# A layer kernel of matrix products: how the first weight slabs are fetched, and what TensorE does until they are there

## The chip, the cores and the metric

The program runs on one core of one Trainium2 chip. The metric is the device time of one execution in microseconds (us); a shorter time is better. The core's engines named here are TensorE (PE in the rows, with its weight loads as PEld), VectorE (DVE), ScalarE (ACT), GpSimd (POOL) and SyncE (SP), which does nothing here but issue transfers (DMA) from the chip's memory (HBM) into the core's own.

## What is computed

One layer over 256 positions of width 2048: an RMS norm, one wide projection, two mixers that run over it in both directions (an mLSTM and a gated DeltaNet), a gated merge with a residual sum, and a feed-forward block of width 8192. Cut from the reference:

```python
def reference(x, norm1_g, w_in, ..., w_branch_m, w_branch_d, w_out, norm2_g, w_ff1, w_ff2, norm_f_g):
    for l in range(DEPTH):                                  # DEPTH = 1
        h = _rms_norm(x, norm1_g[l])
        proj = h @ w_in[l]                                  # 256 x 2048 times 2048 x 11312
        (m_q, m_k, m_v, m_o, m_i, m_f, d_qkv, d_z, d_a, d_b, gates) = jnp.split(proj, split_points, axis=-1)
        y_m = _mlstm_mixer(m_q, m_k, m_v, m_o, m_i, m_f, ...)       # 4 heads
        y_d = _gated_deltanet_mixer(d_qkv, d_z, d_a, d_b, ...)      # conv of 5 taps, 8 heads
        g_m, g_d = jnp.split(gates, 2, axis=-1)
        mixed = jax.nn.sigmoid(g_m) * (y_m @ w_branch_m[l]) + jax.nn.sigmoid(g_d) * (y_d @ w_branch_d[l])
        x = x + mixed @ w_out[l]
        h = _rms_norm(x, norm2_g[l])
        x = x + jnp.square(jax.nn.relu(h @ w_ff1[l])) @ w_ff2[l]
    return _rms_norm(x, norm_f_g)
```

All inputs and the output are float32.

## The kernel before

**Products in three parts.** A large product of float32 is made of three faster ones: each operand is split into a rounded part (`wh`, `xTh`, type fp32r) and the rest (`wl`, `xTl`), and TensorE adds `wh` times `xTh`, `wl` times `xTh` and `wh` times `xTl`. The weights are split on the chip as they arrive, slab by slab.

**Slabs.** A slab (class `Gran`, lines 271 to 299) is two tiles of 128 rows of a weight matrix over one chunk of columns: 288 columns in the first chunk, 512 in nearly all others. SP fetches it into one of NR = 3 buffers `raw` (L286); ScalarE casts it into one of NW = 4 buffers `wh`; VectorE subtracts that from `raw` into `wl`; TensorE then makes 12 products of it: two row tiles, two tiles of positions, three parts. `gemm` (L301) builds the slabs of a chunk, `drive` (L342) runs all slabs of the program in one list. The split of slab i + 3 (its fetch included) is written half-way through the products of slab i. A fetch into `raw` waits until VectorE has read the slab that had the same buffer three slabs earlier.

**The start.** The first chunk is `zab` (288 columns, slabs 0 to 7). Its slabs carry two more steps: `x_load` fetches the rows of the transposed input into `xtr` behind each slab (L382), and `x_prep` (L385) makes `xTh` on ScalarE and `xTl` on VectorE, two operations each a slab, scaled with the norm's gains, which lie in `pr`. `pr` is the first transfer on SP (L379). The second chunk (`d`, 512 columns, slabs 8 to 15) carries `xn_load`: a piece `xn` of the untransposed input behind each slab (L407), and behind the last one the constants `cs`.

**Side work.** Everything that is not a slab is written as tasks: `x_norm` squares the pieces of `xn` into a scratch tile `junk` and makes the root `r1` (its task yields eight squares, a table load and the root on ScalarE, four small steps on VectorE); the chunks `d` are then scaled into `tmd` on ScalarE and transposed by TensorE into `ptd`, and so on through the convolution, both mixers and the gates. A planner places them: `_Clocks` keeps a modelled time for each engine, and at each half slab `pump` takes the tasks whose modelled start is near TensorE's (`pick`). A slab's modelled arrival (`arrive`, in `split`) goes into these times, so it moves the places of side work. The order that comes out is fixed: each engine runs its instructions in the order in which they were written (`keep_in_program_order`), recorded by one helper (L108), so that most rows of the trace carry its line, and the tile's name tells what they are.

**The mLSTM heads.** Much later, around slabs 103 to 112, the heads' scores `sp` are masked into `mm` on VectorE and multiplied on TensorE into `nf` and `nb`, from which VectorE makes `hm`; at the same stretch GpSimd adds masks and VectorE still has every slab's `wl` to make.

Of the kernel before, what the change touches and what calls it, by code (L numbers as in the profile page):

```python
# [9 lines left out]
F32 = mybir.dt.float32  # L10
# [6 lines left out]
P = 128  # L17
# [17 lines left out]
HOP = 0.1  # L35
XNW = 6.0

NR, NW = 3, 4

LIM = dict(T=9, V=2, A=1.2, G=3)  # L40
TABLES = {AF.Sigmoid: "sigmoid", AF.Exp: "exp", AF.Ln: "ln", AF.Sqrt: "sqrt"}
# [98 lines left out]
def layer_kernel(ctx, tc, x, xt, cst, prm, w_in, w_bm, w_bd, w_out, w_ff1, w_ff2, gf, out):  # L140
    nc = tc.nc
    clk = _Clocks()
    V, A, T, G = (_Ordered(tc, e, k, clk) for e, k in
                  ((nc.vector, "V"), (nc.scalar, "A"), (nc.tensor, "T"), (nc.gpsimd, "G")))
# [8 lines left out]
    wp = ctx.enter_context(tc.tile_pool(name="wp", bufs=1))  # L153
# [117 lines left out]
    class Gran:  # L271


        def __init__(self, src, shape, mms, us, pre=None, post=None, prep=None, load=None, segs=2):
            self.src, self.shape, self.mms, self.us = src, shape, mms, us
            self.pre, self.post, self.prep, self.load, self.segs = pre, post, prep, load, segs

        def split(self, i):
            n = int(np.prod(self.shape))
            raw = wp.tile([P, 1024], F32, tag="raw", name="raw", bufs=NR)  # L280
            self.wh = wp.tile([P, 1024], F32R, tag="wh", name="wh", bufs=NW)
            self.wl = wp.tile([P, 1024], F32R, tag="wl", name="wl", bufs=NW)
            rv = raw[:, :n]
            if len(self.shape) == 2:
                rv = rv.rearrange("p (k c) -> p k c", k=self.shape[0])
            nc.sync.dma_start(out=rv, in_=self.src)  # L286
            arrive = (GR[i - NR].ready if i >= NR else 0.0) + 2.3
            arrive = max(arrive, GR[i - 1].arrive if i else 0.0) + n * 512 / 360e3
            if self.load:
                arrive += self.load()  # L290
            self.arrive = arrive
            free = GR[i - NW].end if i >= NW else 0.0
            clk.t["A"] = max(clk.t["A"], free, arrive)
            A.copy(self.wh[:, :n], raw[:, :n])
            clk.t["V"] = max(clk.t["V"], clk.t["A"] + HOP)
            V.tensor_sub(self.wl[:, :n], raw[:, :n], self.wh[:, :n].bitcast(F32))
            if self.prep:
                self.prep()
            self.ready = clk.t["V"] + HOP

    def gemm(w, c0, cw, lh, ll, kt, name, evac, needs=None, pre=None, prep=None, load=None):  # L301

        box = {}

        def mk(g):
            def mms(gr):
                if g == 0:
                    while left["acc"] < 2:
                        force()
                    left["acc"] -= 2  # L310
                    box["ps"] = [ps_acc.tile([P, 512], F32, tag="acc", name=f"{name}_{i}") for i in range(2)]
                for kk in range(2):
                    for t in range(2):
                        k = g + kk
                        ws = slice(kk * cw, (kk + 1) * cw)
                        ts_ = slice(t * P, (t + 1) * P)
                        o = box["ps"][t][:, :cw]
                        h, l = lh()[:, k, ts_], ll()[:, k, ts_]
                        T.matmul(o, h, gr.wh[:, ws], start=(k == 0), stop=False)
                        T.matmul(o, h, gr.wl[:, ws], start=False, stop=False)  # L320
                        T.matmul(o, l, gr.wh[:, ws], start=False, stop=(k == kt - 1))
                    if kk == 0:
# [12 lines left out]
            src = w[g * P:(g + 2) * P, c0:c0 + cw].rearrange("(k p) c -> p k c", p=P)  # L335
            return Gran(src, [2, cw], mms, 12 * cw / 2400 * 1.0125, pre_, post,
                        (lambda: prep(g)) if prep else None, (lambda: load(g)) if load else None)

        for g in range(0, kt, 2):
            GR.append(mk(g))  # L340

    def drive():  # L342
        for i in range(min(LA, len(GR))):
            GR[i].split(i)
        for i, gr in enumerate(GR):
            if gr.pre:
                gr.pre()
            t0 = max(clk.t["T"], gr.ready)
            clk.t["T"] = t0
            seg = gr.us / gr.segs  # L350
            parts = gr.mms(gr)
            gr.end = t0 + gr.us
            for j in range(gr.segs):
                clk.quiet = True
                next(parts, None)
                clk.quiet = False
                clk.t["T"] += seg
                if j == 0 and i + LA < len(GR):
                    pump()
                    gr.end = clk.t["T"] + seg * (gr.segs - 1)  # L360
                    GR[i + LA].split(i + LA)
# [14 lines left out]
    xTh = pa.tile([P, KT, S], F32R, tag="A0", name="xTh")  # L376
    xTl = pa.tile([P, KT, S], F32R, tag="A1", name="xTl")
    xtr = pm.tile([P, KT, S], F32, tag="ba", name="xtr")
    nc.sync.dma_start(out=pr, in_=prm)  # L379

    def x_load(g):
        nc.sync.dma_start(out=xtr[:, g:g + 2, :], in_=xt[:, g:g + 2, :])  # L382
        return 0.75

    def x_prep(g):  # L385
        for k in (g, g + 1):
            A.activation(xTh[:, k, :], xtr[:, k, :], AF.Copy, scale=g1c[:, k:k + 1])
        clk.t["V"] = max(clk.t["V"], clk.t["A"] - 0.3)
        for k in (g, g + 1):
            V.scalar_tensor_tensor(xTl[:, k, :], xtr[:, k, :], g1c[:, k:k + 1], xTh[:, k, :].bitcast(F32),  # L390
                                   op0=ALU.mult, op1=ALU.subtract)

# [2 lines left out]
    NX = DM // 512  # L395
    xl = []

    def xn_load(g):

        i = g // 2  # L400
        if i == 0:
            for t in range(2):
                xn[t] = pm.tile([P, DM], F32, tag=("yd", "hm")[t], name=f"xn{t}")
        t, j = i % 2, i // 2
        if j < NX:
            c = slice(j * 512, j * 512 + 512)
            nc.sync.dma_start(out=xn[t][:, c], in_=x[t * P:(t + 1) * P, c])  # L407
            xl.append(clk.t["A"])
        if g == KT - 2:
            nc.sync.dma_start(out=cs, in_=cst[:, :K_N])  # L410
            return 2.0
        return 0.73
# [7 lines left out]
    def x_norm():  # L420
        ss1 = small.tile([P, 2, NX], F32, name="ss1")
        v = small.tile([P, 2], F32, name="v1")
        junk = pm.tile([P, 512], F32, tag="cm", name="junk")
        for i in range(2 * NX):
            while len(xl) <= i:
                yield None
# [985 lines left out]
    def ff2_gran(pas, ks, ns, last=False, tail=False):  # L1412
# [26 lines left out]
                        mm(g_, ks_, k, 1)  # L1439
                start(ff2_end(1), "end1")  # L1440

        def prep():
# [212 lines left out]
```

## Time and profile before

| | before |
|---|---|
| device time, median of 3 runs (lowest to highest) | 1496.76 us (1496.39 to 1499.19) |
| the profiled execution's own time | 1496.8 us |
| its span in the profile | 1495.0 us |
| TensorE busy, share of the span | 1475.8 us, 99% |
| TensorE's weight loads (beside its products) | 1219.8 us, 82% |
| VectorE | 898.0 us, 60% |
| ScalarE | 781.5 us, 52% |
| GpSimd | 63.4 us, 4% |

The profiled execution took 1.8 us more than its span, which lies around the span and not in it. A share of 99% is a mean over the whole run: it says that an engine is nearly always at work, but not where the rest is lost. That is read from the list of its waits, and for the places it names from a timeline (each instruction with its start, its length and what ended the idle time ahead of it) and from windows (busy time of each engine in a stretch, the granted clock, the share of the 16 DMA engines and the bytes moved).

### The profile page before, as it was taken

The numbers are of one execution on the slowest core, as the hardware profiler recorded it, in microseconds if no ns is written. First come the engines' busy times: TensorE is split into PE (matmuls) and PEld (weight loads), VectorE is DVE, ScalarE is ACT, GpSimd is POOL, SyncE is SP. The second block draws the span as 40 slices with busy tenths as digits, with TensorE's granted clock in tenths as the row PEclk, the third lists the DMA queues.
The fourth block names the chain that finished last, engine by engine and source line by source line (L and its number), as shares of the span: only waits on it lengthen the run. The fifth ranks groups of instructions, "written<-read, shape, count | busy, mean of one in ns | idle before, by whom it ended". The sixth has DMA issues, their size and how long they took to land.

```text
span 1495.0 us, 19315 instructions
## 1 busy us (share of the span) xinstructions
PE 1475.8 (99%) x7196; PEld 1219.8 (82%) x7196; DVE 898.0 (60%) x1292; ACT 781.5 (52%) x1124; POOL 63.4 (4%) x101
## 2 busy tenths in 40 slices
PE   8999999999999999999999999999999999999997
PEld 7888788887878888887888888888888888888886
DVE  5658785368678836565555544454445555555875
ACT  5876545365765455443554444444445444444664
POOL 0020101012001100000000000000000000000000
PEclk9999999999999999999999999999999999999999
DMA  8766477464657754776656666666666666666564
GB/s 290 213 202 199 135 200 213 118 206 145 193 170 203 253 164 127 222 254 235 204 183 194 186 180 188 184 183 195 183 184 186 195 195 191 194 194 194 187 198 140
DMA packets 139805, 286.95 MB, mean 192 GB/s; under 512 B 9588, under 2 KB 18036, under 8 KB 139072
## 3 DMA queue, kind: packets, MB, share of 16 engines
q1 hardware_dynamic: 134816, 267.09, 60.1%
q0 software_dynamic: 4896, 18.64, 3.9%
q8 instruction: 56, 0.92, 0.2%
q14 instruction: 37, 0.30, 0.1%
HBM read 278.32 MB, written 7.36 MB: 191 GB/s over the span
## 4 chain that ended last, share of the span: by engine, by line
PE 90%; DVE 3%; DMA 3%; ACT 2%; issue 1%; DVEq 0%; SPq 0%; ACTq 0%
PE f L108 23%; PE y L108 23%; PE gm L108 6%; PE d L108 6%; PE gd L108 5%; PE wo L108 5%; PE mv L108 3%; PE bd L108 3%; PE bm L108 3%; PE z L108 2%; DMA raw<-in_w_in_dram 2%; PE mq L108 1%; PE mk L108 1%; DVE wl L108 1%; ACT wh L108 1%
## 5 line engine op out<-in xcount | busy, mean ns | idle before, releaser
L108 DVE TENSOR_TENSOR wl<-raw,wh 128x1024 fp32r<-128x1024 f32 (+3 forms) x512 | 611.3, 1196 | 534.2 <-ACT wh L108 533.0
L108 ACT CAST wh<-raw 128x1024 fp32r<-128x1024 f32 (+3 forms) x512 | 523.5, 1026 | 548.4 <-PE y L108 155.0
L108 PE MATMUL f<-wh,h2h 128*128 128x512 f32 x512 | 200.8, 392 | 0.0
L108 PE MATMUL f<-wh,h2l 128*128 128x512 f32 x512 | 199.5, 390 | 0.0
L108 PE MATMUL f<-wl,h2h 128*128 128x512 f32 x512 | 199.2, 389 | 0.0
L108 PE MATMUL y<-wh,ah 128*128 128x512 f32 x512 | 178.5, 389 | 0.0
L108 PE MATMUL y<-wl,ah 128*128 128x512 f32 x512 | 178.5, 389 | 0.0
L108 PE MATMUL y<-wh,al 128*128 128x512 f32 x512 | 178.3, 389 | 0.0
L108 PEld LDWEIGHTS f<-wh,h2l 128*128 128x128 f32 x512 | 96.1, 188 | 20.2
L108 PEld LDWEIGHTS y<-wh,al 128*128 128x128 f32 x512 | 96.1, 188 | 20.0
L108 PEld LDWEIGHTS y<-wl,ah 128*128 128x128 f32 x512 | 96.1, 188 | 20.0
L108 PEld LDWEIGHTS y<-wh,ah 128*128 128x128 f32 x512 | 96.0, 188 | 19.8
L108 PEld LDWEIGHTS f<-wl,h2h 128*128 128x128 f32 x512 | 96.2, 188 | 19.5
L108 PEld LDWEIGHTS f<-wh,h2h 128*128 128x128 f32 x512 | 96.1, 188 | 19.3
L108 PE MATMUL d<-wh,xTh 128*128 128x512 f32 x192 | 78.0, 406 | 0.0
L108 PE MATMUL d<-wl,xTh 128*128 128x512 f32 x192 | 75.2, 391 | 0.6 <-DVE wl L108 0.6
L108 PE MATMUL d<-wh,xTl 128*128 128x512 f32 x192 | 74.9, 390 | 0.0
L108 PE MATMUL gd<-wl,xTh 128*128 128x512 f32 x128 | 50.2, 392 | 1.8 <-DVE wl L108 1.7
L108 PE MATMUL wo<-wh,mTh 128*128 128x512 f32 x128 | 50.6, 395 | 0.2 <-ACT wh L108 0.2
L108 DVE TENSOR_TENSOR al<-aT,ah 128x256 fp32r<-128x256 f32 x128 | 50.8, 417 | 0.0
L108 PE MATMUL wo<-wl,mTh 128*128 128x512 f32 x128 | 50.0, 391 | 0.8 <-DVE wl L108 0.8
L108 PE MATMUL gm<-wh,xTh 128*128 128x512 f32 x128 | 50.6, 395 | 0.0
(316 smaller groups left out, 2153.3 us busy)
## 6 DMA issues: line engine op xcount, KB each, us to landing
raw<-in_w_ff_dram SPq DMA_DIRECT2D x256, 512.0 KB, 4.3
raw<-in_w_in_dram SPq DMA_DIRECT2D x160, 512.0 KB, 3.9
raw<-in_w_out_dram SPq DMA_DIRECT2D x32, 512.0 KB, 4.3
raw<-in_w_bm_dram SPq DMA_DIRECT2D x16, 512.0 KB, 4.2
raw<-in_w_bd_dram SPq DMA_DIRECT2D x16, 512.0 KB, 4.3
raw<-in_w_in_dram SPq DMA_DIRECT2D x16, 256.0 KB, 2.8
mx<-dgm POOLq DMA_DIRECT2D x4, 1024.0 KB, 6.2
raw<-in_w_in_dram SPq DMA_DIRECT2D x8, 288.0 KB, 4.3
```

The source lines that it names most:

```text
L108: return self._tc.keep_in_program_order(f(*a, **k))
```

## The change

The change rewrites how the first slabs are fetched, and adds products of zeros.

- `split` is taken apart: `fetch` issues a slab's transfers, `split` casts and subtracts. `drive` calls `fetch` for the first NF = 8 slabs (the first chunk) ahead of everything else, and with them their `x_load`.
- Slabs 0 to 2 use the three `raw` buffers, slabs 3 to 7 a tile `far` of their own (five slabs of 576 elements a partition) under the tag `cm`, which `junk` had; `junk` gets the tag `pk`.
- Slab 0 is fetched, cast, subtracted and prepared in two halves (one tile of 128 rows each).
- `pr` is issued on ScalarE's queue.
- VectorE sets a tile `zw` of 512 columns to zero, and TensorE runs nine float32 products of 128 x 128 zeros into `zp` ahead of its first real one.
- The planner's model of arrivals is changed with it: the first eight slabs have no wait for a buffer in it.

```diff
+NF = 8
...
+        def fetch(self, i):
+            n = int(np.prod(self.shape))
+
+            if NR <= i < NF:
+                self.raw = far[:, i - NR, :n]
+            else:
+                self.raw = wp.tile([P, 1024], F32, tag="raw", name="raw", bufs=NR)[:, :n]
...
+            arrive = 2.3 + (0.0 if i < NF else GR[i - NF].ready if i < NF + NR else GR[i - NR].ready)
+            arrive = max(arrive, GR[i - 1].arrive if i else 0.0)
+
+            self.at = []
+            for ks in ((0,), (1,)) if i == 0 else ((0, 1),):
+                if i == 0:
+                    nc.sync.dma_start(out=rv[:, ks[0], :], in_=self.src[:, ks[0], :])
+                else:
+                    nc.sync.dma_start(out=rv, in_=self.src)
+                lo, hi = (ks[0] * n // 2, (ks[0] + 1) * n // 2) if i == 0 else (0, n)
+                arrive += (hi - lo) * 512 / 360e3
+                if self.load:
+                    arrive += self.load(ks)
+                self.at.append((ks, lo, hi, arrive))
+            self.arrive = arrive
+
         def split(self, i):
-            n = int(np.prod(self.shape))
-            raw = wp.tile([P, 1024], F32, tag="raw", name="raw", bufs=NR)
+            if i >= NF:
+                self.fetch(i)
+            raw = self.raw
...
-            nc.sync.dma_start(out=rv, in_=self.src)
-            arrive = (GR[i - NR].ready if i >= NR else 0.0) + 2.3
-            arrive = max(arrive, GR[i - 1].arrive if i else 0.0) + n * 512 / 360e3
-            if self.load:
-                arrive += self.load()
-            self.arrive = arrive
...
+            for ks, lo, hi, at in self.at:
+                clk.t["A"] = max(clk.t["A"], free, at)
+                A.copy(self.wh[:, lo:hi], raw[:, lo:hi])
+                clk.t["V"] = max(clk.t["V"], clk.t["A"] + HOP)
+                V.tensor_sub(self.wl[:, lo:hi], raw[:, lo:hi], self.wh[:, lo:hi].bitcast(F32))
+                if self.prep:
+                    self.prep(ks)
...
     def drive():
+        for i in range(NF):
+            GR[i].fetch(i)
...
-    nc.sync.dma_start(out=pr, in_=prm)
...
+    far = pm.tile([P, NF - NR, 576], F32, tag="cm", name="far")
+    nc.scalar.dma_start(out=pr, in_=prm)
+
+
+    zw = pm.tile([P, 512], F32, tag="tmp", name="zw", bufs=4)
+    nc.vector.memset(zw, 0.0)
+    zp = ps_m.tile([P, 512], F32, tag="m", name="zp")
+    for _ in range(9):
+        nc.tensor.matmul(zp[:, 0:128], zw[:, 0:128], zw[:, 128:256], start=True, stop=True)
+
+    def x_load(g, ks):
+        k0, k1 = g + ks[0], g + ks[-1] + 1
+        nc.sync.dma_start(out=xtr[:, k0:k1, :], in_=xt[:, k0:k1, :])
+        return 0.375 * (k1 - k0)
...
-        junk = pm.tile([P, 512], F32, tag="cm", name="junk")
+        junk = pm.tile([P, 512], F32, tag="pk", name="junk", bufs=4)
```

How the program's order moves is shown at three places; L110 in the changed kernel is the helper that was L108.

SP's queue from its first transfer on, in the kernel before, and then in the changed one:

```order
L379 DMA pr<-in_prm_dram 128x209
L286 DMA raw<-in_w_in_dram 128x2x288
L382 DMA xtr<-in_xt_dram 128x512
L286 DMA raw<-in_w_in_dram 128x2x288
L382 DMA xtr<-in_xt_dram 128x512
L286 DMA raw<-in_w_in_dram 128x2x288
L382 DMA xtr<-in_xt_dram 128x512 x2
L286 DMA raw<-in_w_in_dram 128x2x288
```

```order
L296 DMA raw<-in_w_in_dram 128x288
L414 DMA xtr<-in_xt_dram 128x256
L296 DMA raw<-in_w_in_dram 128x288
L414 DMA xtr<-in_xt_dram 128x256
L298 DMA raw<-in_w_in_dram 128x2x288
L414 DMA xtr<-in_xt_dram 128x512
L298 DMA raw<-in_w_in_dram 128x2x288
L414 DMA xtr<-in_xt_dram 128x512
L298 DMA far<-in_w_in_dram 128x2x288
L414 DMA xtr<-in_xt_dram 128x512
```

`pr` has left the queue, slab 0 and its rows of `xtr` come in two pieces, and from the fourth slab on the target is `far`.

ScalarE from the cast ahead of the last squares (slab 18's before, slab 17's in the changed kernel) to the first scalings `tmd`, after which TensorE's first transposes `ptd` can run, before and then changed (`ss` takes a square's sum, `rs` is the root of `x_norm`):

```order
L108 CAST wh<-raw 128x1024
L108 ACTIVATE junk,ss_326<-xn_269 128x512
L108 ACTIVATE junk,ss_326<-xn_270 128x512
L108 CAST wh<-raw 128x1024 x2
L108 ACT_TABLE_LOAD
L108 ACTIVATE rs<-v_327 128x2
L108 CAST wh<-raw 128x1024
L108 ACTIVATE tmd<-d_0_318,r_79 128x512
L108 ACTIVATE tmd<-d_1_319,r_79 128x512
```

```order
L110 CAST wh<-raw 128x1024
L110 ACTIVATE junk,ss_338<-xn_280 128x512
L110 ACTIVATE junk,ss_338<-xn_279 128x512
L110 ACTIVATE junk,ss_338<-xn_280 128x512
L110 CAST wh<-raw 128x1024 x2
L110 ACT_TABLE_LOAD
L110 ACTIVATE rs<-v_339 128x2
L110 CAST wh<-raw 128x1024
L110 ACTIVATE tmd<-d_0_330,r_79 128x512
L110 ACTIVATE tmd<-d_1_331,r_79 128x512
```

The last squares, the table load and the scalings `tmd` all stand one cast earlier in the program. On TensorE the first four `ptd` stood half into slab 19 and four more half into slab 21; now all eight stand half into slab 18.

VectorE where the mLSTM heads' masked scores `mm` end and the head sums `nf` and `nb` are used, before and then changed (`wl` is a slab's subtraction):

```order
L108 TENSOR_TENSOR mm<-sp,mm 128x128 x2
L108 TENSOR_TENSOR mm<-sp,mm 128x256
L108 TENSOR_TENSOR wl<-raw,wh 128x1024
L108 TENSOR_TENSOR mm<-sp,mm 128x256
L108 TENSOR_TENSOR mm<-sp,mm 128x128 x2
L108 TENSOR_TENSOR mm<-sp,mm 128x256
L108 COPY dn<-nf 128x1
L108 COPY dn<-nb 128x1
L108 SCALAR_TENSOR_TENSOR dn<-dn 128x2
L108 TENSOR_TENSOR dn<-dn,emc 128x2
```

```order
L110 TENSOR_TENSOR mm<-sp,mm 128x128 x2
L110 TENSOR_TENSOR mm<-sp,mm 128x256
L110 COPY dn<-nf 128x1
L110 COPY dn<-nb 128x1
L110 SCALAR_TENSOR_TENSOR dn<-dn 128x2
L110 TENSOR_TENSOR dn<-dn,emc 128x2
L110 RECIPROCAL dn<-dn 128x2
L110 TENSOR_SCALAR hm<-nf,dn 128x256
L110 SCALAR_TENSOR_TENSOR hm<-nb,dn,hm 128x256
L110 TENSOR_TENSOR wl<-raw,wh 128x1024
```

The subtraction that stood between the last scores stands now behind `hm`. On TensorE the products that belong to these rows stood at slabs 107 to 110 and stand now at slabs 103 to 105.

## Rows read from the trace of the kernel before

**Rows 1.** TensorE's waits, whole run: total us, times, longest us.
```profile
PE zab L108 <- ACT xTh L108: 5.8, 1, 5.8
...
PE gd L108 <- DVE wl L108: 1.7, 2, 1.3
```

**Rows 2.** Timeline of TensorE, first 30 us: start, length, what, [idle before <- by].
```profile
5.78 0.61 PE L108 MATMUL zab<-wh,xTh 128*128 128x288 f32 x1 [5.78 <-ACT xTh L108]
...
9.70 0.44 PE L108 MATMUL zab<-wh,xTh 128*128 128x288 f32 x1
9.94 0.37 PE L108 MATMUL zab<-wl,xTh 128*128 128x288 f32 x1
10.28 0.29 PE L108 MATMUL zab<-wh,xTh 128*128 128x288 f32 x1
10.41 0.29 PE L108 MATMUL zab<-wl,xTh 128*128 128x288 f32 x1
...
21.77 0.40 PE L108 MATMUL d<-wh,xTh 128*128 128x512 f32 x1
22.72 0.50 PE L108 MATMUL d<-wl,xTh 128*128 128x512 f32 x1 [0.56 <-DVE wl L108]
...
28.08 0.39 PE L108 MATMUL d<-wh,xTh 128*128 128x512 f32 x1
```

**Rows 3.** Timeline of ScalarE and VectorE: casts of slabs 0, 8; subtraction of slab 8.
```profile
4.50 0.67 ACT L108 CAST wh<-raw 128x576 fp32r<-128x576 f32 x1 [2.47 <-DMA raw<-in_w_in_dram]
...
20.36 1.05 ACT L108 CAST wh<-raw 128x1024 fp32r<-128x1024 f32 x1 [0.45 <-DVE xTl L108]
...
21.44 1.22 DVE L108 TENSOR_TENSOR wl<-raw,wh 128x1024 fp32r<-128x1024 f32 x1 [0.76 <-ACT wh L108]
```

**Rows 4.** Chain of waits, first 60 us: start us, us, what.
```profile
5.99 4.51 DMA raw<-in_w_in_dram
...
19.92 6.15 DMA raw<-in_w_in_dram
...
27.25 1.24 DVE wl L108
...
28.54 24.57 PE d L108 x107
```

**Rows 5.** Timeline of SP's queue: when a transfer is issued, us it takes SP.
```profile
6.41 0.47 SPq L382 DMA_DIRECT2D xtr<-in_xt_dram  x1
...
15.07 0.37 SPq L286 DMA_DIRECT2D raw<-in_w_in_dram  x1
```

**Rows 6.** Windows: us, busy (x) of PE PEld DVE ACT POOL, PEclk, DMA share, GB/s.
```profile
0.00:4.00 4.00, 0.00 (x0) 0.00 (x0) 0.00 (x0) 1.28 (x1) 0.34 (x6) 1.00 0.49 130
4.00:10.49 6.49, 4.71 (x20) 4.61 (x21) 4.47 (x9) 4.74 (x9) 0.00 (x0) 1.00 1.01 340
10.49:26.07 15.58, 15.03 (x94) 13.24 (x93) 10.30 (x18) 9.52 (x17) 0.00 (x0) 1.00 0.94 302
23.00:28.00 5.00, 5.00 (x23) 4.11 (x23) 1.97 (x2) 2.09 (x2) 0.00 (x0) 1.00 1.02 350
340.00:372.00 32.00, 29.48 (x133) 22.72 (x135) 30.07 (x70) 16.43 (x30) 9.48 (x10) 1.00 0.50 150
```

**Rows 7.** Timeline of TensorE: small products in float32.
```profile
69.46 1.04 PE L108 MATMUL pr_c<-masks,gd 128*8 128x128 f32 x8
```

**Rows 8.** Timeline of ScalarE and TensorE, 42 to 55 us: ahead of the first transposes.
```profile
42.57 1.05 ACT L108 CAST wh<-raw 128x1024 fp32r<-128x1024 f32 x1 [0.57 <-DMA raw<-in_w_in_dram]
...
50.84 1.28 ACT L108 ACT_TABLE_LOAD   x1
...
54.04 1.26 ACT L108 ACTIVATE tmd<-d,r 128x512 f32<-128x512 f32 x2
54.06 0.39 PE L108 MATMUL d<-wh,xTl 128*128 128x512 f32 x1
...
54.78 0.66 PE L108 MATMUL ptd<-cs,tmd 128*128 128x128 f32 x4 [0.33 <-ACT tmd L108]
```

More of the change, by code (lines that the diff above doesn't have):

```diff
@@ L276, in __init__ @@
             self.pre, self.post, self.prep, self.load, self.segs = pre, post, prep, load, segs
+        def fetch(self, i):
[4 more added lines that the diff above has]
+                self.raw = wp.tile([P, 1024], F32, tag="raw", name="raw", bufs=NR)[:, :n]
+            rv = self.raw
+            if len(self.shape) == 2:
+                rv = rv.rearrange("p (k c) -> p k c", k=self.shape[0])
+            arrive = 2.3 + (0.0 if i < NF else GR[i - NF].ready if i < NF + NR else GR[i - NR].ready)
[12 more added lines that the diff above has]
+            self.arrive = arrive
@@ L278, in split @@
         def split(self, i):
-            n = int(np.prod(self.shape))
-            raw = wp.tile([P, 1024], F32, tag="raw", name="raw", bufs=NR)
+            if i >= NF:
+                self.fetch(i)
+            raw = self.raw
             self.wh = wp.tile([P, 1024], F32R, tag="wh", name="wh", bufs=NW)
             self.wl = wp.tile([P, 1024], F32R, tag="wl", name="wl", bufs=NW)
-            rv = raw[:, :n]
-            if len(self.shape) == 2:
-                rv = rv.rearrange("p (k c) -> p k c", k=self.shape[0])
@@ L286, in split @@
-            nc.sync.dma_start(out=rv, in_=self.src)
-            arrive = (GR[i - NR].ready if i >= NR else 0.0) + 2.3
-            arrive = max(arrive, GR[i - 1].arrive if i else 0.0) + n * 512 / 360e3
-            if self.load:
-                arrive += self.load()
-            self.arrive = arrive
-            free = GR[i - NW].end if i >= NW else 0.0
-            clk.t["A"] = max(clk.t["A"], free, arrive)
-            A.copy(self.wh[:, :n], raw[:, :n])
-            clk.t["V"] = max(clk.t["V"], clk.t["A"] + HOP)
@@ L296, in split @@
-            V.tensor_sub(self.wl[:, :n], raw[:, :n], self.wh[:, :n].bitcast(F32))
-            if self.prep:
-                self.prep()
+            free = GR[i - NW].end if i >= NW else 0.0
+            for ks, lo, hi, at in self.at:
[5 more added lines that the diff above has]
+                    self.prep(ks)
@@ L336, in mk @@
             return Gran(src, [2, cw], mms, 12 * cw / 2400 * 1.0125, pre_, post,
-                        (lambda: prep(g)) if prep else None, (lambda: load(g)) if load else None)
+                        (lambda ks: prep(g, ks)) if prep else None, (lambda ks: load(g, ks)) if load else None)
         for g in range(0, kt, 2):
@@ L378, in layer_kernel, with x_prep @@
     xtr = pm.tile([P, KT, S], F32, tag="ba", name="xtr")
-    nc.sync.dma_start(out=pr, in_=prm)
[L381 to L386, printed above, removed]
+    far = pm.tile([P, NF - NR, 576], F32, tag="cm", name="far")
[9 more added lines that the diff above has]
+        return 0.375 * (k1 - k0)
+    def x_prep(g, ks):
+        for k in [g + j for j in ks]:
             A.activation(xTh[:, k, :], xtr[:, k, :], AF.Copy, scale=g1c[:, k:k + 1])
         clk.t["V"] = max(clk.t["V"], clk.t["A"] - 0.3)
-        for k in (g, g + 1):
+        for k in [g + j for j in ks]:
             V.scalar_tensor_tensor(xTl[:, k, :], xtr[:, k, :], g1c[:, k:k + 1], xTh[:, k, :].bitcast(F32),
@@ L396, in layer_kernel, with xn_load @@
     xl = []
-    def xn_load(g):
+    def xn_load(g, ks):
         i = g // 2
@@ L1440, in mms, with prep @@
                 start(ff2_end(1), "end1")
-        def prep():
+        def prep(_):
             for k in ks:
```

## The prediction

> **What bounds the kernel now.** I read the page first, then TensorE's waits, then the first 60 us as a timeline, then the bytes moved by stretch. The page's shares (in the table above) say that TensorE is busy 99% of the span. The list of its waits is short: 5.8 us before the first product, and behind that no single wait above 1.3 us [rows 1]. So only what lies ahead of TensorE at the start, or opens new waits, can move the time. The profiled execution took 1496.8 us, the median of the runs is 1496.76, so the sum below is made on 1496.8.
>
> The start reads like this. TensorE's first product stands at 5.78. The products of 288 columns start 0.24 us apart until about 9.9 and 0.13 apart from 10.28 on [rows 2]: 288 columns in 0.24 us is the lower level, 1.2 GHz, although the clock column prints 1.00 there [rows 6]. The first chunk (8 slabs, 96 products) ends at 21.77; at full pace it is 96 x 0.131 = 12.6 us, and it took 16.0. Then the second product of the next chunk stands only at 22.72 [rows 2], because the `wl` of slab 8 ends at 22.66 [rows 3]; and behind the first product of slab 10 (28.08) the next comes at 28.54 and not 0.23 later. From there 107 products run without a break [rows 2, 4]. So the question for the start is: how much earlier are slab 8 and slab 10 split?
>
> What stands ahead of the split? The chain of waits runs through transfers, that of slab 3 (4.51 us) and that of slab 10 (6.15 us) among them [rows 4]. SP's queue shows why they start late: a slab waits for one of three `raw` buffers, so that slab 3 is issued only at 5.99 and slab 10 at 19.92 [rows 4], slab 8 at 15.07 [rows 5]. But the transfers are slow too, and the bytes say why: 340 GB/s at a share of 1.01 of the 16 DMA engines from 4 to 10.49, and still 302 GB/s (0.94) from 10.49 to 26.07 [rows 6]. They are near their ceiling almost throughout; waiting for buffers wastes only the small rest. That limits what issuing early can bring.
>
> **The slabs issued at once, the term that counts.** Slabs are numbered from 0; one of the first chunk is 0.295 MB, its rows of `xtr` 0.262, a slab of 512 columns 0.524, its piece of `xn` 0.262, `pr` 0.107. By [rows 6], 4 x 0.130 = 0.52 MB had moved by 4.0, 0.52 + 6.49 x 0.340 = 2.73 by 10.49, and 2.73 + 15.58 x 0.302 = 7.43 by 26.07. Asked for through slab 3 (four pieces of `xtr` issued ahead of it) was 0.107 + 4 x 0.295 + 4 x 0.262 = 2.34 MB, and it landed at 10.5 [rows 4]: a transfer counts as landed when 0.39 MB more than itself and all ahead of it have moved. For slab 10, landed at 26.07: asked 0.107 + 8 x (0.295 + 0.262) + 3 x 0.524 + 2 x 0.262 = 6.66, trailing 0.77. After the change the queue holds the same bytes in nearly the same order with no wait through slab 10, since `far` takes slabs 3 to 7, and slabs 8 to 10 take buffers that slabs 0 to 2 left long ago. Through slab 8 that is 5.09 MB. It lands when 5.48 to 5.86 MB have moved, at 340 GB/s from 4.0 on at 18.6 to 19.7; I take 19.2, the middle, as neither trailing is nearer. Its cast started at 20.36 before [rows 3], so cast, `wl` and TensorE's second product come **1.15 us** earlier (0.65 to 1.75). At 350 GB/s, the best five microseconds of the start [rows 6], it would land at 18.2 to 19.3 and the gain reach 2.2.
>
> Slab 10 then lands at 23.2 to 24.3; with 1.05 for the cast and 1.24 for `wl` [rows 3, 4] it is split by 26.6, and TensorE asks for that at 22.72 - 1.15 + 24 x 0.2285 = 27.05. So the wait there goes, 0.46 - 0.23 = **0.23 us**. From slab 11 on three buffers bind as before: a slab with its piece of `xn` is 0.79 MB, 2.3 us at 340 GB/s, below TensorE's 2.74 for 12 products.
>
> The Trainium skill, in DMA: Bandwidth & Descriptors, section Where 436 GB/s comes from, gives about 358 GB/s as what one core gets from HBM, more than the 340 of the row. By that figure slab 8 would land about 0.8 us earlier (an estimate), and the time would be 1494.6; the measured rate decides here.
>
> **The zero products.** No row shows them. The nearest are the eight rows `pr_c`, float32 of 128 columns, 1.04 us with the tail of the last, thus 0.11 apart [rows 7]; the program has four such products there, so one costs 0.22, and twice that at the lower clock: nine cost 2.0 to 4.0 us. They wait for a memset of 512 columns on VectorE, which no row shows either: above 0, and at most about 0.6 us, half a subtraction over 1024 columns [rows 3]. TensorE is idle until 5.78 anyway. Started after 0.75 they end by 5.4 at the latest and cost at most a microsecond of waiting for a first half slab that is ready at about 4.5. That microsecond is hidden: 12.6 us of products from 5.4 on end at 18.0, and slab 7 with its rows (4.57 MB asked) lands only at 17.1 to 18.2 and must be prepared after that. If the clock rose no sooner than before, 17 products at 0.11 extra would add 1.9 us, to 19.9, still ahead of the second product of slab 8 at 21.6. So this part counts **0**; were the transfers not the bound, it would be worth those 1.9 us.
>
> **Halves, queue and tiles.** The halves add one cast and one subtraction; a half cast costs between half of 0.67 and the whole [rows 3], so both together add at most 0.7 us to engines that then wait for the next slab; they only bring the first product forward: 0. SP issues its 18 transfers at 0.4 to 0.5 us each [rows 5] without waiting, and is done by about 9, ahead of the transfers themselves: 0. `pr` goes to ScalarE's queue; no row shows a transfer issued there, SP's take 0.4 to 0.5 [rows 5]. With the table load of 1.28 behind it [rows 8], from 0.74 on, ScalarE is free by 2.5, and its first cast came at 4.50 [rows 3]; an issue would have to cost over 2 us to be seen: 0.
>
> **The order behind.** The planner's clocks start earlier, so it places side work 1 to 7 slabs earlier; TensorE's work stays the same. Two places can change. (a) The first transposes `ptd` stood half into slab 19 and lost 0.49 us on `tmd` (54.06 to 54.78 instead of 0.23) [rows 8]. Now eight stand half into slab 18, which TensorE reached at 51.55 and will reach at 51.55 - 1.38 = 50.2. ScalarE's chain to them, from the cast of slab 17 on, is by the order four casts (4.2), three squares (2.3), the table (1.28), the root with VectorE's steps (1.5) and a first scaling (0.65): 10 us. That cast started at 42.57 before [rows 8], 1.5 to 2 sooner now: `tmd` at 50.5 to 51. I count the same 0.5 lost: 0, bounds -0.5 to +1. (b) From 340 to 372 TensorE idled 2.5 us [rows 6], in part on `wl` [rows 1], where the mLSTM heads crowd VectorE. They now stand four slabs earlier and one subtraction tighter, with the same operations: 0, bounds -2.5 to +2.5.
>
> Sum: 1496.8 - 1.15 - 0.23 = **1495.4**.
>
> **The rivals.** *TensorE's pace sets the first chunk*: it starts at 5.0 on the full clock and ends at 17.6 instead of 21.77; with the 0.23 that is 1492.4. For it speaks that 16 products ran at half pace. Against it: slab 8 would have to land by 16.2, at least 4.96 MB in 12.2 us or 407 GB/s, and the best row has 350 [rows 6]. The Trainium skill has the mechanism in TensorE: Matmul & The Clock Gate, section What's actually happening: activity releases the throttle, so zero products would raise the clock for the real ones. *The crowd of 340 to 372 dissolves* in the new order: another 2.5 off, 1492.9; *or it doubles*: 1497.9. *The transposes come too early*, the case on the slower side: if the eight squares and the table load are no sooner done than before, `tmd` comes at 54.7 again; TensorE waits for it with one slab (2.74) less done than before and four transposes (0.44) more, 2.3 behind: 1499.1. It decides where `tmd` comes after 52.4; my chain says 50.5 to 51.
>
> **How the numbers follow.** Forecast 0.52 (its own range 1494.4 to 1496.2), full pace 0.07, crowd gone 0.16, crowd doubled 0.12, transposes too early 0.13. 0.2% is 3.0 us, about what a measurement of this kernel can tell from no change. Faster by more (below 1493.8): full pace, most of crowd gone, a tail of the forecast, 0.23. Slower by more (above 1499.8): the worse half of the early transposes and a tail, 0.07. Within: 0.70. The range reaches into both neighbours, 1492.4 to 1498.2.
>
> **What would show it.** Slab 8's cast at 18.6 to 19.7; the DMA share at 1.0 from 3 to 20 us; a first product near 5 and a pause of over a microsecond ahead of the second product of slab 8, at about 21.6; no wait at slab 10. I am wrong if that product stands before 20.5 (transfers faster than 350), if `ptd` waits over 2 us, or if the idle time from 340 to 372 moves by more than 2.

## The result and the profile after

The changed kernel takes **1506.66 us** (median of 4 runs, 1505.81 to 1509.52) where the kernel before takes 1497.16 on the same chip: 1.0065 times as long, 95% interval 1.0053 to 1.0076. It is 9.5 us slower; 1.4 us faster was forecast. The profiled execution took 1505.81 us, its span is 1504.0. One run of a kernel below (e1) took 2191.32 us at a granted clock of 0.64 and is left out of its ratio.

Some tile names below: `cacc` is the convolution ahead of the DeltaNet mixer, `pq` the sums of its squares and `sr` a copy of these, `cmd` the DeltaNet mask, `pk` and `po` an early and the last product of a DeltaNet group of heads, `gm` a chunk of gate columns and `sgm` its sigmoid.

The start went better than forecast. TensorE's timeline (start, length, what, idle before and its releaser):

```profile
1.46 4.21 PE L410 MATMUL zp<-zw 128*128 128x128 f32 x18 [1.46 <-DVE zw L407]
5.33 0.59 PE L110 MATMUL zab<-wh,xTh 128*128 128x288 f32 x1
...
5.95 0.41 PE L110 MATMUL zab<-wh,xTl 128*128 128x288 f32 x1
6.19 0.30 PE L110 MATMUL zab<-wh,xTh 128*128 128x288 f32 x1
6.33 0.29 PE L110 MATMUL zab<-wl,xTh 128*128 128x288 f32 x1
...
20.18 0.40 PE L110 MATMUL d<-wh,xTh 128*128 128x512 f32 x1
20.42 0.48 PE L110 MATMUL d<-wl,xTh 128*128 128x512 f32 x1
```

The second product of slab 8 stands at 20.42 and not at 22.72 [rows 2]; the first real products start 0.24 apart, up to 6.19, and then 0.13 apart, but for gaps of 0.2 to 0.4 up to 9.15. In the chain of waits (start, us, what) no transfer is left behind that of the second slab, slab 1, and the pause at slab 10 [rows 4] is gone: TensorE runs without a break from 20.34 to the first transposes, which come with no wait either [rows 8].

```profile
2.60 4.38 DMA raw<-in_w_in_dram
...
8.16 12.18 PE zab L110 x84
20.34 28.68 PE d L110 x126
49.03 1.11 PE ptd L110 x8
```

So by 50 us the changed kernel is 2.3 + 0.23 us ahead for the start and 0.5 for the transposes. Then it loses all that and 9.5 us more. TensorE's waits, whole run (total us, times, longest), beside the short list of before [rows 1]:

```profile
PE pq L110 <- ACT cacc L110: 2.7, 2, 1.5
PE d L110 <- DVE wl L110: 2.4, 1, 2.4
PE ptd L110 <- ACT tmd L110: 1.8, 1, 1.8
PE gm L110 <- DVE wl L110: 1.6, 4, 0.8
```

Two of these places show how. First 78 to 85 us, ScalarE and TensorE: the cast of slab 31 waits 3.95 us for its transfer, `cacc` stands in the queue behind it, and TensorE waits for `cacc`.

```profile
82.64 1.05 ACT L110 CAST wh<-raw 128x1024 fp32r<-128x1024 f32 x1 [3.95 <-DMA raw<-in_w_in_dram]
83.60 1.05 ACT L110 ACTIVATE cacc<-kqd 128x1024 f32<-128x1024 f32 x1
...
84.70 0.64 PE L110 MATMUL pq<-cacc,cs 128*32 128x256 f32 x8 [1.48 <-ACT cacc L110]
```

Second the stretch of the mLSTM heads, 343 to 351 us, VectorE, GpSimd and TensorE: while GpSimd adds its masks, a pair of `cacc` steps on VectorE takes 1.91 and the next 3.00 us instead of 0.87, and the subtraction `wl` behind them comes 2.4 us late.

```profile
341.65 0.87 DVE L110 SCALAR_TENSOR_TENSOR cacc<-cp,pr,cacc 128x256 f32<-128x256 f32 x2
343.57 1.91 DVE L110 SCALAR_TENSOR_TENSOR cacc<-cp,pr,cacc 128x256 f32<-128x256 f32 x2
346.57 3.00 DVE L110 SCALAR_TENSOR_TENSOR cacc<-cp,pr,cacc 128x256 f32<-128x256 f32 x2
349.49 1.21 DVE L110 TENSOR_TENSOR wl<-raw,wh 128x1024 fp32r<-128x1024 f32 x1
...
343.60 5.69 POOL L110 TENSOR_TENSOR cmd<-cmd,cs 128x512 f32<-128x512 f32 x4 [1.50 <-DMA cmd<-dcr]
...
350.76 0.67 PE L110 MATMUL d<-wl,xTh 128*128 128x512 f32 x1 [2.40 <-DVE wl L110]
351.23 0.63 PE L110 MATMUL d<-wh,xTl 128*128 128x512 f32 x1
```

### The profile page after: what moved, and what is told of

It reads as the page before. It is cut to its first block, busy times and chain, and to the rows that moved or that the text cites. A ratio compares the mean times of both kernels' runs of the same rounds, so it can differ in the third digit from the quotient of the medians.

```text
span 1504.0 us, 19344 instructions
## 1 busy us (share of the span) xinstructions
PE 1481.5 (99%) x7214; PEld 1223.1 (81%) x7214; DVE 897.7 (60%) x1294; ACT 779.2 (52%) x1123; POOL 62.3 (4%) x101
## 4 chain that ended last, share of the span: by engine, by line
PE 84%; DVE 7%; DMA 5%; ACT 2%; issue 1%; SPq 0%; DVEq 0%; ACTq 0%
PE f L110 23%; PE y L110 23%; PE wo L110 6%; PE gd L110 6%; PE d L110 5%; DMA raw<-in_w_in_dram 4%; PE mv L110 3%; PE bd L110 3%; PE gm L110 3%; DVE wl L110 3%; PE bm L110 2%; PE mk L110 1%; PE mq L110 1%; PE z L110 1%; DVE cacc L110 1%
## 5 line engine op out<-in xcount | busy, mean ns | idle before, releaser
L110 DVE TENSOR_TENSOR wl<-raw,wh 128x1024 fp32r<-128x1024 f32 (+3 forms) x508 | 606.2, 1196 | 530.3 <-ACT wh L110 529.3
L110 ACT CAST wh<-raw 128x1024 fp32r<-128x1024 f32 (+3 forms) x508 | 520.4, 1028 | 549.6 <-PE y L110 159.3
L110 PE MATMUL f<-wh,h2h 128*128 128x512 f32 x512 | 200.8, 392 | 0.0
L110 PE MATMUL f<-wh,h2l 128*128 128x512 f32 x512 | 199.5, 390 | 0.0
L110 PE MATMUL f<-wl,h2h 128*128 128x512 f32 x512 | 199.2, 389 | 0.0
L110 PE MATMUL y<-wh,ah 128*128 128x512 f32 x512 | 178.5, 389 | 0.0
L110 PE MATMUL y<-wl,ah 128*128 128x512 f32 x512 | 178.5, 389 | 0.0
L110 PE MATMUL y<-wh,al 128*128 128x512 f32 x512 | 178.4, 389 | 0.0
L110 PEld LDWEIGHTS f<-wh,h2l 128*128 128x128 f32 x512 | 96.1, 188 | 20.1
L110 PEld LDWEIGHTS y<-wh,al 128*128 128x128 f32 x512 | 96.1, 188 | 20.1
L110 PEld LDWEIGHTS y<-wl,ah 128*128 128x128 f32 x512 | 96.1, 188 | 20.0
L110 PEld LDWEIGHTS y<-wh,ah 128*128 128x128 f32 x512 | 96.0, 188 | 19.7
L110 PEld LDWEIGHTS f<-wl,h2h 128*128 128x128 f32 x512 | 96.2, 188 | 19.5
L110 PEld LDWEIGHTS f<-wh,h2h 128*128 128x128 f32 x512 | 96.1, 188 | 19.4
L110 PE MATMUL d<-wl,xTh 128*128 128x512 f32 x192 | 75.7, 394 | 2.4 <-DVE wl L110 2.4
L110 PE MATMUL d<-wh,xTh 128*128 128x512 f32 x192 | 77.7, 405 | 0.0
L110 PE MATMUL d<-wh,xTl 128*128 128x512 f32 x192 | 75.6, 394 | 0.0
L110 PE MATMUL gm<-wl,xTh 128*128 128x512 f32 x128 | 50.4, 394 | 1.6 <-DVE wl L110 1.6
L110 PE MATMUL gd<-wh,xTh 128*128 128x512 f32 x128 | 51.1, 399 | 0.0
L110 DVE TENSOR_TENSOR al<-aT,ah 128x256 fp32r<-128x256 f32 x128 | 50.8, 417 | 0.0
L110 PE MATMUL wo<-wh,mTh 128*128 128x512 f32 x128 | 50.5, 394 | 0.0
L110 PE MATMUL gm<-wh,xTh 128*128 128x512 f32 x128 | 50.1, 392 | 0.2 <-ACT wh L110 0.2
```

The lines of the kernel that those rows point to most:

```text
L110: return self._tc.keep_in_program_order(f(*a, **k))
```

## The experiments

Two theories to begin with. **Order**: the planner, told of an earlier start, put the side work elsewhere, and the new places lose the time. **Fetch**: the new fetching itself leaves something behind that costs later. All ratios are to the kernel before, run on the same chip.

**Fetch and order apart.** The planner reads only `arrive`; the transfers obey only the code. So each can be had without the other. e1 has the new fetching with the old model (the halves of slab 0 are booked as one):

```diff
-            arrive = 2.3 + (0.0 if i < NF else GR[i - NF].ready if i < NF + NR else GR[i - NR].ready)
+            arrive = 2.3 + (0.0 if i < NF else GR[i - NR].ready)
...
+            if i < NF:
...
+                arrive = (GR[i - NR].ready if i >= NR else 0.0) + 2.3
+                arrive = max(arrive, GR[i - 1].arrive if i else 0.0) + n * 512 / 360e3
...
```

e2 has the old fetching with the new model (slab 0 is booked in halves):

```diff
-            arrive = (GR[i - NR].ready if i >= NR else 0.0) + 2.3
+            arrive = 2.3 + (0.0 if i < NF else GR[i - NF].ready if i < NF + NR else GR[i - NR].ready)
...
```

> The changed kernel with all of its fetching, halves and zero products, but the planner is told the arrivals it was told before, so that behind the first chunk every engine runs its work in the order of the kernel before. Theory 'order' (the new places of the side work cost the time, the start gains 2.5 us: second product of slab 8 at 20.4 instead of 22.7, no wait at slab 10): 1494.5 us, 1493.5 to 1495.5. Theory 'fetch' (something that the new fetching leaves behind, tiles or transfers, makes the later waits): 1505 to 1507, with the waits at 297, 350, 514 and 577 us still there.

> The kernel before with its own fetching, but the planner is told the arrivals of the changed kernel, so that behind the first chunk every engine runs in the changed order. Theory 'order': the loss without the gain at the start, 1509 us, 1507.5 to 1510.5. Theory 'fetch': as before, 1496 to 1498.

e1: **1494.31 us**, ratio 0.9982 (0.9972 to 0.9991), 2.8 us faster than before (1497.12). e2: **1511.09**, ratio 1.0100 (1.0086 to 1.0114), 14 us slower. In the traces each side product of TensorE stands at the same slab in e1 as in the kernel before, and in e2 as in the changed one. Fetch falls, order stands: the new fetching is worth 2.8 us in the old order and 4.4 in the new, and the new order costs 12 to 14. e1 beats both kernels. Its waits, behind the zero products, are nearly those of before:

```profile
PE gd L110 <- DVE wl L110: 1.7, 2, 1.3
PE zp L436 <- DVE zw L433: 1.5, 1, 1.5
PE pq L110 <- ACT cacc L110: 1.2, 1, 1.2
PE nf L110 <- DVE hm L110: 0.7, 1, 0.7
```

The spans of the changed kernel and e1 differ by 1504.0 - 1492.4 = 11.6 us. Adding up by how much products behind the first chunk start later than usual (over 0.3 us each, and eight slow products in a row) gives 16.8 in the changed kernel and 5.7 in e1, so these account for 11.1 of the 11.6: 1.6 at 82.8, 1.1 at 96 and 105, 2.0 at 297, 0.8 at 337, 4.2 at 350 (2.6 of wait, then eight products 0.43 apart), 1.4 at 362, 1.0 at 428, 2.5 at 486 to 516, 2.3 at 572 to 582. TensorE reaches the second DeltaNet group's `pk` at 407.75 in the changed kernel and at 432.96 in e1; ahead of that 11.1 are lost and 5.0, behind it 5.7 and 0.7.

**The zero products.** e1 without them:

```diff
-    zw = pm.tile([P, 512], F32, tag="tmp", name="zw", bufs=4)
-    nc.vector.memset(zw, 0.0)
-    zp = ps_m.tile([P, 512], F32, tag="m", name="zp")
-    for _ in range(9):
-        nc.tensor.matmul(zp[:, 0:128], zw[:, 0:128], zw[:, 128:256], start=True, stop=True)
```

> As e1 (new fetching, old order), without the nine zero products and their memset. If the zero products only fill idle time (transfers set the first chunk): same time as e1 within 0.3 us, the second product of slab 8 still at 20.4. If they raise the clock ahead of the real products and TensorE sets the first chunk: some 16 products at 0.24 instead of 0.13, first chunk ends 1 to 1.9 us later (21.2 to 22.1 instead of 20.2), time up by as much less what the transfers of slabs 9 and 10 hide: 0.5 to 1.9 us above e1.

1494.63 us, ratio 0.9985 (0.9976 to 0.9994): not to be told from e1. The trace shows what they do: without them the first product stands at 4.60, some 20 products start about 0.24 apart (the 1.2 GHz level), until 10.86, and the first chunk ends at 20.91 instead of 20.47; in e1 the 0.24 ends at 6.91. So TensorE comes to the higher level sooner behind them, and they are worth 0.4 us of trace, less than the 1 to 1.9 expected. The times can't resolve it, and the traces hardly: that chunk ends anywhere from 20.17 to 20.66 in twelve traces with zero products, and at 21.59 in h2 below.

```profile
4.60 0.61 PE L110 MATMUL zab<-wh,xTh 128*128 128x288 f32 x1 [4.60 <-ACT xTh L110]
...
10.62 0.44 PE L110 MATMUL zab<-wh,xTl 128*128 128x288 f32 x1
10.86 0.39 PE L110 MATMUL zab<-wh,xTh 128*128 128x288 f32 x1
11.08 0.30 PE L110 MATMUL zab<-wl,xTh 128*128 128x288 f32 x1
```

**What the new places run into.** Two suspects: the mask broadcasts on GpSimd's queue (1.5 MB each), which hold slabs back, and the mask additions on GpSimd, which slow VectorE. Three kernels leave most of them out; the planner is told nothing of it, so the order stays. In m2 and m3 (new order) and m4 (old order, new fetching) the broadcasts are cut to 8 columns a piece:

```diff
-        G.dma_start(out=cm[:, :, 0:256], in_=rows(0, 0, 256))
...
+        G.memset(cm, -3.0e4)
...
+        G.dma_start(out=cm[:, :, 0:8], in_=rows(0, 0, 8))
...
```

In m3 and m4 the additions are cut to 8 columns a block as well:

```diff
-                G.tensor_add(v[:, :, b, :], v[:, :, b, :],
-                             cs[:, kc:kc + 128].unsqueeze(1).broadcast_to([P, 4, 128]))
...
+                G.tensor_add(v[:, :, b, 0:8], v[:, :, b, 0:8],
+                             cs[:, kc:kc + 8].unsqueeze(1).broadcast_to([P, 4, 8]))
```

> The changed kernel in its own order; of the three mask broadcasts (GpSimd's queue, 1.5 MB each: cmd, mm, cmd again) only 8 of 128 to 256 columns of each piece are moved, the rest of the tile is set to a large negative number by GpSimd beforehand, so that part of the mixers' weights is zero. Theory 'late slabs': these transfers hold back the slabs, and the ScalarE steps that TensorE waits for stand behind the cast of the late slab (waits of 1.64 at 82.8 and 2.0 at 297.4): both go, 1503 us (1502 to 1504). Rival 'crowded engines' (the waits come from the order on ScalarE and VectorE alone, the transfers are on time or hidden): unchanged, 1506 to 1507.

> As the run before, and the mask additions on GpSimd cover 8 columns instead of 128 a block (the masks are left out of the rest). Theory: these additions slow VectorE down (two cacc steps took 3.00 us beside them, 0.87 without), and with it the wait of 2.56 at 350.8 (and the eight products behind it at 0.43 us instead of 0.23, 1.6 us) and the one of 1.39 at 362: they go too, 1498 us (1497 to 1500). Rival: the additions are not what makes VectorE late there: no more than 1 us below the run before.

> New fetching in the order of the kernel before (1494.3), with the same things left out as in the run before. If the two orders differ because the new one meets the broadcasts and the additions at worse places, the distance of 12.4 us between them shrinks to the 4 to 5 us of waits at 428, 486, 514 and 577, which these do not touch: 1491 to 1494 here. If the orders differ for other reasons, this one gains as much as the new order does and the distance stays near 12.

m2: 1503.36 us, ratio 1.0047 (1.0028 to 1.0065). m3: 1498.75, ratio 1.0013 (1.0003 to 1.0022). Both medians are as forecast: 3.3 us for the broadcasts, 4.6 for the additions. The 7.9 together are clear of the noise; the 3.3 alone are not, since m2's interval overlaps that of the changed kernel (1.0053 to 1.0076). The mechanism is there in each trace, though not wait for wait: the one at 82.8 falls in m2 from 1.64 to 0.78 and is not gone, and in m3 the wait for `cacc` that stood at 362 stays, at 1.25. From 70 to 83 us a slab of 512 columns takes 6.1 us from issue to landing in the changed kernel and 3.8 in m2 (line of the transfers: count, KB, us to landing; the changed kernel first):

```profile
raw<-in_w_in_dram SPq DMA_DIRECT2D x2, 512.0 KB, 6.1
cmd<-dcr POOLq DMA_DIRECT2D x2, 512.0 KB, 6.4
```

```profile
raw<-in_w_in_dram SPq DMA_DIRECT2D x2, 512.0 KB, 3.8
...
cmd<-dcr POOLq DMA_DIRECT2D x4, 16.0 KB, 3.9
```

In m3 the pairs of VectorE steps that took 1.91 and 3.00 beside GpSimd's additions take 0.88:

```profile
339.72 0.88 DVE L110 SCALAR_TENSOR_TENSOR cacc<-cp,pr,cacc 128x256 f32<-128x256 f32 x2
340.51 0.27 DVE L110 TENSOR_SCALAR ssm<-ssm 128x8 f32<-128x8 f32 x1
340.59 0.88 DVE L110 SCALAR_TENSOR_TENSOR cacc<-cp,pr,cacc 128x256 f32<-128x256 f32 x2
341.38 1.22 DVE L110 TENSOR_TENSOR wl<-raw,wh 128x1024 fp32r<-128x1024 f32 x1
```

In the Trainium skill, SBUF — State Buffer, section SBUF: two separate sides, VectorE and GpSimd share a pair of ports that one instruction holds to its end, and a VectorE step with two inputs in that memory is among those that need it when GpSimd reads there too; these rows agree, with 1.91 and 3.00 us beside the additions and 0.88 without them.

m4 was a miss: 1489.91, ratio 0.9950 (0.9934 to 0.9967). The old order gains 4.4 us by the same cuts. So the distance between the orders shrinks only from 12.4 to 8.8 us: the broadcasts and additions hurt both, the new order by 3.5 us more. Four kernels stand behind that figure, and their intervals together are about as wide as it is. They are at most a part of the answer, not the whole.

**Three casts put elsewhere.** If single places made the waits, moving a cast or two would cure them. In the new order the cast of slab 31 goes behind `cacc`, that of slab 98 behind `tmd`, that of slab 178 ahead of eight squares (`place` writes a slab's cast and subtraction, `begin` its fetch).

```diff
+LATE, EARLY = (31, 98), (178,)
...
+                    if i + LA - 1 in LATE:
+                        GR[i + LA - 1].place()
...
+            if i + LA + 1 in EARLY:
+                GR[i + LA + 1].begin(i + LA + 1)
+                GR[i + LA + 1].place()
```

> The changed kernel with three casts of slabs put elsewhere on ScalarE (with their subtractions on VectorE), everything else in its order: the cast of slab 31 behind the cacc step that it stood ahead of, that of slab 98 behind the scalings tmd, that of slab 178 ahead of the eight squares jkd. Theory 'place': the waits at 82.8 (1.64), 297.4 (2.0) and 572 to 582 (2.3 in four pieces) come from these three places alone, a cast that waits for its late slab or one that stands behind squares and so holds its buffer; they go: 1501 us (1500 to 1502.5). Rival 'crowd': the engines are short of time there, so what is won at one instruction is lost at the next: 1505 to 1507.

1505.49 us, ratio 1.0056 (1.0043 to 1.0070): 1.2 us won of 5.9, too little to tell from none (the changed kernel: 1.0053 to 1.0076). The waits at 82.8 and 297 did go, but the first came back at once as a wait for `sr`, which stands behind the late slab's subtraction on VectorE, and the 2.0 us won at 297 were gone again by 365: the crowd of 345 to 365 ended no earlier (a wait of 1.75 where 1.20 was, and the granted clock at 0.83 from 360 to 370).

```profile
87.43 0.44 PE L111 MATMUL pc<-cs,sr 128*128 128x128 f32 x2 [1.24 <-DVE sr L111]
...
348.78 0.50 PE L111 MATMUL d<-wl,xTh 128*128 128x512 f32 x1 [2.44 <-DVE wl L111]
```

Only slab 178 paid, and little: TensorE is 1.0 us ahead of the changed kernel at 516 and 2.05 at 582 (first product of the chunk in between at 575.68 instead of 577.23), but a wait of 0.76 stays behind that product. "Crowd" is nearer the truth than "place": what stands too close together is late at one instruction or at the next.

**Other orders from the same planner.** What makes one order slow? The fetching stays that of the changed kernel in all of these; one number of the planner's model is changed, the modelled rate of the first 11 slabs (v1 330, v2 300, v3 310, v4 500 GB/s in place of 360) or the modelled delay between engines (h1 0.15, h2 0.20, h3 0.50 us in place of 0.10). v1 and h1 stand for their kind:

```diff
-                arrive += (hi - lo) * 512 / 360e3
+                arrive += (hi - lo) * 512 / (330e3 if i < NF + NR else 360e3)
...
-HOP = 0.1
+HOP = 0.15
```

> The changed kernel with one number of the planner's model changed: the first 11 slabs are modelled at 330 instead of 360 GB/s. The fetching is the same; 44% of the side products on TensorE change place by more than 0.4 slab. Theory 'an early start makes a bad order': slower arrivals in the model lead back toward the old time by a part, and the order stays close to 1506 (1504 to 1507). Rival 'the order is a draw': any small change of the model draws another order, with a time anywhere between 1494 and 1511, and off 1506.7 by more than 2 us.

> The changed kernel; the planner's model moves the first 11 slabs at 300 GB/s instead of 360 (70% of TensorE's side products stand elsewhere than in the changed and in the old order). Theory 'draw': one more order, its time not told by the model's rate: anywhere from 1494 to 1511, off the next run by over 2 us. Rival 'an earlier modelled start makes a worse order' (1506.7 at 360, 1502.4 at 330): 1497 to 1500, and close to the next run.

> As the run before with 310 GB/s: the planner then lands within 10% of the places of the old order. Theory 'draw': near the old order with the new fetching, 1494 to 1497. Rival: between the runs at 300 and 330, 1498 to 1501.

> The changed kernel; the planner's model moves the first 11 slabs at 500 GB/s instead of 360. A third of TensorE's side products stand elsewhere than in the changed kernel; the places of the late work are the same (heads' products at slab 103.5, the second group's pk at 127.5, po at 175; in the old order 108, 142.5 and 186). Theory 'the earlier the model starts, the further ahead side work is put, and the more it crowds' (300: 1496.2, 310: 1494.5, 330: 1502.4, 360: 1506.7): 1505 to 1510, with waits near 345 to 362 and 570 to 580 again. Theory 'draw': off 1506.7 by more than 2.5 us on the faster side, with no wait above 1 us in one of these two places.

> The changed kernel with its own modelled arrivals; the planner's delay from one engine to the next is 0.15 us instead of 0.10, which puts the late side work back where the old order had it (heads at slab 108.5, second group's pk at 143.5, po at 185; in the changed kernel 103.5, 127.5, 175; in the old order 108, 142.5, 186), though 54% of all side products stand elsewhere than in the old order. Theory 'far ahead': the time goes with these places, 1494 to 1497. Rival 'the modelled start': the arrivals are those of the changed kernel, so 1504 to 1508.

> The same with a delay of 0.20: heads late (109), but the second group still further ahead than in the changed kernel (pk at 126, po at 168). If the second group's place makes the loss: 1503 to 1510, with waits above 1 us between 400 and 600. If the heads' place makes it: 1494 to 1499.

> The same with a delay of 0.50: everything later than in the old order (heads at 118.5, pk at 150, po at 196). Theory 'far ahead': no crowd, 1492 to 1497, unless the work then stands so late that the output projection has to wait for it (a wait ahead of the chunks bd or wo); in that case 1497 or more with that wait in the trace. Rival 'the modelled start': 1504 to 1508.

The results, with the slab at which TensorE comes to the heads' head sums (`nf`), to the second DeltaNet group's `pk` and to its `po`:

| kernel (all with the new fetching) | heads | pk | po | us | ratio to before |
|---|---|---|---|---|---|
| e1, old order | 108 | 142.5 | 186 | 1494.31 | 0.9982 |
| v3, 310 | 108 | 142.5 | 186 | 1494.48 | 0.9977 |
| v2, 300 | 107.5 | 140.5 | 180 | 1496.21 | 0.9993 |
| h1, delay 0.15 | 108.5 | 143.5 | 185 | 1496.45 | 1.0000 |
| v1, 330 | 104.5 | 130 | 175 | 1502.43 | 1.0037 |
| changed kernel, 360 | 103.5 | 127.5 | 175 | 1506.66 | 1.0065 |
| v4, 500 | 103.5 | 127.5 | 175 | 1508.17 | 1.0064 |
| h2, delay 0.20 | 109 | 126 | 168 | 1508.43 | 1.0075 |
| h3, delay 0.50 | 118.5 | 150 | 196 | 1513.28 | 1.0110 |

Neither theory holds throughout. "A draw" had v1 and v3 right, missed v2 (1.7 us from v3, not over 2) and v4; "earlier start" had v4 right, and v1, v2 and v3 came out faster than it gave. And the modelled start is not the cause as such: h1 keeps it and has the late work back in its old place, and runs 10 us faster than the changed kernel, with 54% of all side products elsewhere than in the old order. Over these kernels the time goes with the place of the second group: all four kernels that reach `pk` at slab 140 to 144 take 1494 to 1497, all four that reach it at 126 to 130 take 1502 to 1509. h2 shows that the heads' place is not needed for that: they stand late there, and it is slow all the same. Its dearest wait is for the heads' `hm`, behind the second group's work:

```profile
477.34 0.45 PE L110 MATMUL pty<-cs,hm 128*128 128x128 f32 x1 [4.85 <-DVE hm L110]
```

h3 shows the other end, at another chunk than I had named: with everything late, the next product of a gate chunk has to wait until the sigmoid `sgm` has read sums made before, and TensorE waits for 8 us.

```profile
616.00 0.79 PE L110 MATMUL gm<-wh,xTh 128*128 128x512 f32 x1 [8.08 <-ACT sgm L110]
```

## Why the prediction was wrong

**The start: right in kind, half its size.** The term of 1.15 us measured 2.30, the 0.23 at slab 10 came as said. The product that was to stand at 21.6 stood at 20.42, before the 20.5 that I had named as a sign of being wrong. The mis-sized step is the rate: I carried 340 GB/s [rows 6] into a queue that no longer waits. Windows of the changed kernel over the same stretch (columns as in [rows 6]) show 330 up to 10.49, but then

```profile
8.00:14.00 6.00, 5.95 (x39) 5.26 (x39) 5.64 (x12) 5.43 (x13) 0.00 (x0) 1.00 1.06 386
14.00:20.00 6.00, 6.00 (x47) 6.00 (x46) 5.43 (x11) 4.64 (x9) 0.00 (x0) 1.00 1.05 398
```

A share of 1.01 at 340 GB/s had looked like a ceiling; with more transfers queued the same 16 engines move 17% more at 1.05. Slab 8 landed at 18.0 (19.2 forecast, 18.6 to 19.7 the bounds), as its cast on ScalarE and its subtraction on VectorE show:

```profile
18.03 1.05 ACT L110 CAST wh<-raw 128x1024 fp32r<-128x1024 f32 x1 [0.44 <-DMA raw<-in_w_in_dram]
...
19.12 1.23 DVE L110 TENSOR_TENSOR wl<-raw,wh 128x1024 fp32r<-128x1024 f32 x1 [0.57 <-ACT wh L110]
```

The rate of 358 GB/s that I had cited from the Trainium skill as one core's share, DMA: Bandwidth & Descriptors, section Where 436 GB/s comes from, is exceeded too, by the 398 of this trace. The Trainium skill, in the same page's section Measured, has 425 for transfers of 16 MB that GpSimd issues on a core alone. The 398 here lies between the two.

**The rival of full pace: half true.** The pause that I expected ahead of slab 8's second product isn't there: from 9 us on TensorE ran at full pace with hardly a pause, so it, not the transfers, ended the first chunk, at 20.18, and the `wl` of slab 8 was there at 20.35, just in time for 20.42. The rival had 17.6; up to 9 us TensorE still waited for the splits of the first two slabs (slab 1 landed at 6.98), and its first products ran at half pace.

**Zero products, halves, `pr`, `far`: right, as far as tested.** They were counted at nothing; the zero products bring 0.4 us, too little for the times to show. No run takes the halves, `pr` and `far` apart from the rest of the fetching. SP issued the last of its 18 transfers at 11.05 and not by 9, which cost nothing that can be seen.

**The transposes (a): right.** They were given 0, bounds -0.5 to +1, and gained 0.5; the rival "too early" didn't occur. But the place is tight: in m2, whose program is the same up to there, the trace has `ptd` wait 1.0 us.

**The crowd of the heads (b): past its bound of 2.5.** It was counted at 0. Against e1, the waits and the slow products from 337 to 362 cost the changed kernel 6.4 us where e1 has 2.9 (0.85, 1.42 and 0.61) at the same work: 3.5 more.

**The step that failed: "Two places can change."** I looked at the two places where TensorE had waited before and took the rest to stay free of waits, since it had been so. But the planner had moved the second group by 11 to 15 slabs, where I had put 1 to 7 for all side work, and the work around it with it. Waits that were in no row of before, at 82.8, 96 to 105, 297, 428, 486 to 516 and 572 to 582, add up to 10.4 us, against 2.8 in e1 outside the heads' crowd (0.67, 1.45, 0.68). None of my rivals had a loss by places not yet seen; the largest went to 1499.1. The order of the changed kernel lay open: the place of `pk` and `po` could have been read there, and the range should have been wider for it.

**What stays open.** That the order costs 12 to 14 us is shown. That some 3.5 of these come from GpSimd's broadcasts and additions is likely: the slowed steps are in the trace, but the figure is as small as its noise. That the second group's place goes with the time is shown over the eight upper rows of the table, not why. It can be a mark of the order more than its cause, since about half of what the changed kernel loses against e1 is lost ahead of `pk`, and the last row, with the latest place, is the slowest. Two more things are open: slabs that land late around 505 to 514 (8.7 us in the median, beside `mx`, the gates read back on GpSimd's queue) and casts behind squares at 560 to 565 are seen in the trace, and only the latter was tested, with about 1 us regained.

## What to carry to other kernels

A change at the start of a kernel whose order a planner computes is two changes: time the new code in the old order and the new order with the old code, before judging either. Where one engine is busy 99%, an edit that moves the side work between its products can only be cheap or dear by the waits that it opens. How large a share moves says little: 840 of 1052 side products of TensorE stand at other slabs than before in the changed kernel, and as many in v2, which takes 1496.21 us. Look at how far whole groups of that work moved, not only at the places that waited before. Keep the good order (here: keep the planner's old arrivals, e1), and take the gain of the start by itself.

## What the runs showed of the hardware

- From 8 to 20 us transfers issued ahead moved 386 to 398 GB/s on this core; with three buffers handed back one by one, 291 to 303 in the same microseconds. From 4 to 10.49 issuing ahead brought nothing: 330 against 340 [rows 6]. The kernel before (columns as in [rows 6]):

```profile
8.00:14.00 6.00, 6.00 (x40) 6.00 (x40) 5.24 (x12) 5.20 (x11) 0.00 (x0) 1.00 0.92 291
14.00:20.00 6.00, 6.00 (x42) 5.34 (x40) 4.21 (x9) 4.03 (x9) 0.00 (x0) 1.00 0.95 303
```

- Beside GpSimd's four additions over 512 columns (5.69 us), a pair of VectorE steps of 256 columns went from 0.87 to 1.91 and 3.00 us.
- A wait of 2.40 us at 348 was followed by eight products 0.43 apart (granted clock 0.66 from 350 to 355), a wait of 2.44 at the same place in s1 by products 0.23 apart (granted clock 1.00): much the same pause was followed by the lower level, 1.2 GHz, in one run and not in the other.

```profile
350.00:355.00 5.00, 4.24 (x12) 3.38 (x13) 4.83 (x13) 0.00 (x0) 0.00 (x0) 0.66 0.37 105
```
